# Routing heads and gate stage of a hybrid block: candidates put together a head later, early gathers by half-heads, first product dealt out by contraction steps

## The chip, the cores and the metric

The kernel runs on one core of one Trainium2 chip. The metric is the device time of one execution in microseconds (us), taken as the median of several runs; a profile comes from one further execution.

The engines are named as in the profile: PE is TensorE (PEld its weight loads), DVE is VectorE, ACT is ScalarE, POOL is GpSimd, SP is the engine whose queue issues most loads. Each engine works through its own list of instructions in order and stops at the first one whose inputs or buffers are not ready.

## The reference, cut to what matters

One layer on 512 tokens of 1024 numbers: a normalised mixing block (gating group and banded attention), added to the input, and then a PEER block, which is added too. The change touches the PEER block alone.

```python
def peer_ffn(x, w_query, sub_keys, expert_u, expert_v):
    tokens = x.reshape(-1, 128, d)
    def block(xb):
        q = (xb @ w_query).reshape(128, 8, 2, 128)          # 8 heads, 2 halves
        sc = einsum('thpd,hpkd->thpk', q, sub_keys)         # 128 keys per half
        s_top, i_top = lax.top_k(sc, 16)
        cand = s_top[:, :, 0, :, None] + s_top[:, :, 1, None, :]
        cand_idx = i_top[:, :, 0, :, None] * 128 + i_top[:, :, 1, None, :]
        best, pos = lax.top_k(cand.reshape(128, 8, 256), 16)
        eidx = take_along_axis(cand_idx.reshape(128, 8, 256), pos, -1)
        g = softmax(best, -1)
        u = take(expert_u, eidx, axis=0)                    # 16384 experts of 1024
        h = gelu(einsum('thkd,td->thk', u, xb))
        vv = take(expert_v, eidx, axis=0)
        return einsum('thk,thkd->td', g * h, vv)
```

So every token picks 16 of 16384 experts in each of 8 heads.

## The kernel before, in words

Token tiles have 128 tokens; there are four. Three of them (384 tokens) are computed densely, the first tile by gathering. For the dense tokens the kernel multiplies *all* experts: a first product (x by expert_u, GELU), multiplied by a dense table of gates, and a second product with expert_v. Of those 384 tokens the last 64 are an exception: their first product is not dense (the first product has 320 columns, `NDU`); instead the rows of expert_u that they chose are gathered "early". 64 tokens times 128 choices make 64 gathers of 128 rows, since partitions 64 to 127 hold one half of the choices of these tokens and partitions 0 to 63 the other half.

Experts are worked in tiles of 128, two tiles to a chunk. A tile of the first product is 8 contraction steps (`KT`); each step is three matmuls on a split of the float32 operands into a high and a low part (`mm3`). Before a tile can be multiplied, SP loads it (`raw`), ACT copies the high part (`hi`, L122), and DVE or POOL subtracts to get the low part (`lo`, L123).

Two stages matter here.

The **head stage** (about 225 to 448 us) has one turn per head. `candidates(h)` loads and splits a 1024 by 256 piece of w_query, multiplies it (tiles `pa`), copies the query out (`qt`, ACT L629), multiplies it by the keys (L637), copies the scores out (`scr`, ACT L640) and lets DVE find the 16 best keys of each half (`best_keys`, L551 to L555, tiles `top` and `pos`). Between, it multiplies two tiles of the first product (`pu`, evacuated by ACT as `act`, L534). `pairs` turns the positions into numbers (ACT L568, L569) and adds up the 50 candidates of a head (DVE L576, tile `cand`). In the next turn `choose` finds the 16 best candidates (DVE, tiles `gate` and `bpos`), fills `tree` with copies (POOL L583), makes the bit masks (DVE L589) and picks the expert numbers by six predicated copies (L601) and a copy into `eidx` (L603). Every second turn `indices_early` brings the numbers of two heads for the last 64 tokens into `eu` (a POOL DMA, L494, and an ACT copy, L495); `ready_early` converts them to integers on ACT (L499); `gather_early` issues up to six gathers a turn on POOL (L479, tile `rowe`, 8 buffers), and `dots_early` multiplies each landed row by x and sums (DVE L488). The turns are traced in program order, and a scheduler then sets the order on each engine by priority and by when it expects inputs to be ready. After the last head come eight tiles of the first product as a bridge.

The **gate stage** (about 454 to 635 us) builds the dense table of gates, 8 tokens a step, 48 steps: DVE compares numbers (`bm` L717, `am` L727), POOL multiplies `bm` by the gate (L719), ACT makes two of eight slices of `am`, PE multiplies (L740, into `pa`), ACT copies out (`gst`, L743) and every two steps stores 1 MB to DRAM (L746). `bm` and `am` have three buffers, and PE works two steps behind (`LEAD`). One early gather is issued in each step while some are left, and its dot follows three steps later. Between, 14 tiles of the first product are multiplied: two in the first step and then one whole tile every fourth step, set by `here`, and each multiplied tile is followed by the split of the next. Here the order on PE, DVE, ACT and POOL is the order of the code (`manual_schedule`). After it come six more tiles, and then the second product, which is not changed.

## Time and profile before

| what | value |
|---|---|
| median of 3 runs (lowest, highest) | 1500.43 us (1500.3, 1507.03) |
| the profiled execution's own time | 1508.44 us |
| its span, first to last instruction | 1506.3 us |
| mean granted TensorE clock | 0.978 |
| busy: PE, DVE, ACT, POOL | 1410.9, 1151.1, 645.4, 682.8 us |
| chain that ended last, by engine | PE 35%, DVE 23%, DMA 19%, issue 13%, POOL 7%, ACT 3% |

Read it by stages: PE is busy in 94% of the span, but the second product makes up more than half of that; in the two stages of the change other engines and the DMA take turns at the limit. The profiled execution is 8.0 us longer than the median, and its span is 2.1 us shorter than its time.

### The profile page before, as it was taken

The page shows a single profiled execution, that of the slowest core. Times are in us where ns is not written, and L with a number is a line of the kernel's source. Part 1 is how long each engine was busy: PE and PEld are TensorE (multiplying, and loading weights), DVE is VectorE, ACT ScalarE, POOL GpSimd, SP SyncE. Part 2 cuts the span into 40 slices and gives each one's busy share as a digit, 9 for nine tenths or more (in the row PEclk, how much of TensorE's full clock was granted, in tenths as well). Part 3 has the DMA queues.
Part 4 walks back from the last instruction along what each step waited for, and adds up shares of the span by engine and source line. Part 5 has one row for each costly group of instructions (what it writes and reads, how often), then busy time and mean ns, then how long its engine had stood idle before and what let it go on. Part 6 is the DMA issues. An engine that isn't in the chain of part 4 may idle for free.

```text
span 1506.3 us, 21702 instructions
## 1 busy us (share of the span) xinstructions
PE 1410.9 (94%) x7804; PEld 1241.8 (82%) x7804; DVE 1151.1 (76%) x2345; ACT 645.4 (43%) x1116; POOL 682.8 (45%) x458
## 2 busy tenths in 40 slices
PE   7999999979888788999979999999999999999998
PEld 6886678968877787988968889989898989888877
DVE  4437553779987996578979798898798888788883
ACT  5447534323336766743434333343333333333331
POOL 0000016567748996403525455454555645344520
PEclk9999999989999998999999999999999999999999
DMA  5352225366747996777878899999999999879992
GB/s 181 112 182 70 84 101 194 121 244 217 250 148 220 336 336 184 208 282 276 291 280 294 318 351 343 346 360 348 369 342 349 367 354 377 318 281 328 331 343 99
DMA packets 160907, 396.77 MB, mean 263 GB/s; under 512 B 11792, under 2 KB 74016, under 8 KB 158752
## 3 DMA queue, kind: packets, MB, share of 16 engines
q1 hardware_dynamic: 62992, 197.42, 37.1%
q0 software_dynamic: 46976, 171.50, 30.8%
q10 hardware_dynamic: 50832, 26.48, 6.1%
q8 instruction: 61, 1.00, 0.3%
q14 instruction: 46, 0.38, 0.1%
HBM read 363.86 MB, written 31.46 MB: 262 GB/s over the span
## 4 chain that ended last, share of the span: by engine, by line
PE 35%; DVE 23%; DMA 19%; issue 13%; POOL 7%; ACT 3%; ACTq 0%; DVEq 0%; SPq 0%; POOLq 0%
DMA row<-in_vd,eint 7%; DMA row<-in_ud,eint 6%; PE pu L138 4%; PE pu L140 4%; PE pu L139 4%; DVE lo L123 4%; PE pa L138 3%; PE pa L139 3%; PE pa L140 3%; DVE rowe L488 3%; DVE row L851 2%; PE pa L918 2%; PE pa L919 2%; PE pa L922 2%; POOL row L860 2%
## 5 line engine op out<-in xcount | busy, mean ns | idle before, releaser
L122 ACT ACTIVATE hi<-raw 128x1024 fp32r<-128x1024 f32 x300 | 317.3, 1059 | 508.4 <-DMA raw<-in_vd 194.0
L123 DVE TENSOR_TENSOR lo<-raw,hi 128x1024 fp32r<-128x1024 f32 x251 | 311.4, 1242 | 114.1 <-ACT hi L122 113.2
L860 POOL DMA_INDIRECT row<-in_vd,eint x128 | 201.6, 1575 | 194.7 <-DVE acc L862 159.9
L849 POOL DMA_INDIRECT row<-in_ud,eint x128 | 177.0, 1383 | 201.7 <-DVE row L851 157.4
L140 PE MATMUL pu<-xch,lo 128*128 128x320 f32 x816 | 252.9, 310 | 9.1 <-DVE lo L123 7.1
L138 PE MATMUL pu<-xch,hi 128*128 128x320 f32 x816 | 254.7, 312 | 2.6 <-ACT act L534 2.2
L139 PE MATMUL pu<-xcl,hi 128*128 128x320 f32 x816 | 252.6, 310 | 0.0
L918 PE MATMUL pa<-hi,wh 128*128 128x512 f32 x512 | 200.8, 392 | 0.0
L919 PE MATMUL pa<-lo,wh 128*128 128x512 f32 x512 | 200.2, 391 | 0.0
L862 DVE SCALAR_TENSOR_TENSOR acc<-row,hw,acc 128x1024 f32<-128x1024 f32 x128 | 165.1, 1290 | 42.5 <-DMA row<-in_vd,eint 40.8
L851 DVE SCALAR_TENSOR_TENSOR row<-row,xb 128x1024 f32<-128x1024 f32 x128 | 155.9, 1220 | 36.1 <-DMA row<-in_ud,eint 34.4
L140 PEld LDWEIGHTS pu<-xch,lo 128*128 128x128 f32 x816 | 154.5, 189 | 10.2 <-DVE lo L123 7.9
L138 PEld LDWEIGHTS pu<-xch,hi 128*128 128x128 f32 x816 | 154.8, 190 | 5.8 <-ACT act L534 3.4
L922 PE MATMUL pa<-hi,wl 128*128 128x512 f32 x512 | 158.1, 390 | 0.0
L139 PEld LDWEIGHTS pu<-xcl,hi 128*128 128x128 f32 x816 | 154.5, 189 | 1.6
L123 POOL TENSOR_TENSOR lo<-raw,hi 128x1024 fp32r<-128x1024 f32 x49 | 118.6, 2434 | 79.3 <-ACT hi L122 79.0
L740 PE MATMUL pa<-bm,am 128*128 128x128 f32 x768 | 100.5, 289 | 27.5 <-POOL bm L719 14.5
L740 PEld LDWEIGHTS pa<-bm,am 128*128 128x128 f32 x768 | 94.7, 201 | 32.8 <-POOL bm L719 26.8
L918 PEld LDWEIGHTS pa<-hi,wh 128*128 128x128 f32 x512 | 96.8, 189 | 20.6
L919 PEld LDWEIGHTS pa<-lo,wh 128*128 128x128 f32 x512 | 96.7, 189 | 20.4
L922 PEld LDWEIGHTS pa<-hi,wl 128*128 128x128 f32 x512 | 96.5, 188 | 20.5
L919 PE MATMUL px<-lo,wh 128*128 128x512 f32 x256 | 101.2, 395 | 9.2 <-DVE lo L123 9.1
(216 smaller groups left out, 2620.6 us busy)
## 6 DMA issues: line engine op xcount, KB each, us to landing
raw<-in_uT SPq DMA_DIRECT2D x128, 512.0 KB
raw<-in_vd SPq DMA_DIRECT2D x128, 512.0 KB
gd<-gst ACTq DMA_DIRECT2D x24, 1024.0 KB
gc<-gd SPq DMA_DIRECT2D x15, 1536.0 KB
raw<-in_w_in SPq DMA_DIRECT2D x20, 512.0 KB
raw<-in_wq SPq DMA_DIRECT2D x16, 512.0 KB
raw<-in_w_out SPq DMA_DIRECT2D x8, 512.0 KB
bt<-in_bias SPq DMA_DIRECT2D x8, 256.0 KB
```

The lines of the kernel that those rows point to most:

```text
L122: nc.scalar.activation(hi, raw, AF.Copy)
L123: eng.tensor_tensor(lo, raw, hi.bitcast(F32), op=ALU.subtract)
L138: nc.tensor.matmul(ps, lh[0], rh[0], start=first, stop=False)
L139: nc.tensor.matmul(ps, lh[0], rh[1], start=False, stop=False)
L140: nc.tensor.matmul(ps, lh[1], rh[0], start=False, stop=last)
L740: nc.tensor.matmul(ps[:, i * P:(i + 1) * P], am[:, 4 * q + i, :], bm[:, 4 * q + i, :], start=True, stop=True)
L849: nc.gpsimd.indirect_dma_start(out=row, out_offset=None, in_=ud, in_offset=bass.IndirectOffsetOnAxis(ap=eint[:, j:j + 1], axis=0))
L851: nc.vector.scalar_tensor_tensor(row, row, 1.0, xb0, op0=ALU.mult, op1=ALU.mult, accum_out=hw[:, j:j + 1])
L860: nc.gpsimd.indirect_dma_start(out=row, out_offset=None, in_=vd, in_offset=bass.IndirectOffsetOnAxis(ap=eint[:, j:j + 1], axis=0))
L918: nc.tensor.matmul(accs[t][half], wh[:, b, tok], w[b][0][:, ds_], start=first, stop=False)
L919: nc.tensor.matmul(accs[t][half], wh[:, b, tok], w[b][1][:, ds_], start=False, stop=False)
L922: nc.tensor.matmul(accs[t][half], wl[:, b, tok], w[b][0][:, ds_], start=False, stop=last)
```

## The change

Three edits. `candidates` returns the best keys, and `pairs` is called in the next turn, just ahead of `choose`. The early gathers go by half-heads: the numbers are written as integers straight into `eui`, one half by a converting POOL DMA and the other by a POOL copy, in every turn for the head before, and seven gathers a turn instead of six; the order of the choices in `du` and `dots` follows. And the first product in the gate stage is no longer dealt out by tiles but by contraction steps: `multiply_some` multiplies as many steps of the open tile as the rest needs per remaining step of the loop, and keeps two split tiles ahead (`HELD`).

```diff
-EARLY = 6
+EARLY = 7
+HELD = 2
...
         def indices_early(h):
-            js = slice(h // 2 * TOPK, (h // 2 + 1) * TOPK)
-            nc.gpsimd.dma_start(eu[0:P - UX, js], eidx[P - UX:P, TT - 1, (h + 1) * TOPK:(h + 2) * TOPK])
-            nc.scalar.copy(eu[P - UX:P, js], eidx[P - UX:P, TT - 1, h * TOPK:(h + 1) * TOPK])
+            js = slice(h * HK, (h + 1) * HK)
+            nc.gpsimd.dma_start(eui[0:P - UX, js], eidx[P - UX:P, TT - 1, h * TOPK + HK:(h + 1) * TOPK])
+            nc.gpsimd.tensor_copy(eui[P - UX:P, js], eidx[P - UX:P, TT - 1, h * TOPK:h * TOPK + HK])
         def ready_early(h):
-            js = slice(h // 2 * TOPK, (h // 2 + 1) * TOPK)
-            nc.scalar.copy(eui[:, js], eu[:, js])
-            early.extend(range(js.start, js.stop))
+            early.extend(range(h * HK, (h + 1) * HK))
...
+        def multiply_some(n, whole=False):
+            x2 = (xbh[:, :, T0:T0 + NDU], xbl[:, :, T0:T0 + NDU]) if whole else (xch, xcl)
+            while n > 0 and (open_tile or ready):
+                if not open_tile:
+                    open_tile.extend((*ready.pop(0), pu(), 0))
+                c, b, (hi, lo), ps, k0 = open_tile
+                k1 = min(KT, k0 + n)
+                for k in range(k0, k1):
+                    mm3(ps[:, :NDU], (hi[:, k, :], lo[:, k, :]), [v[:, k, :] for v in x2], k == 0, k == KT - 1)
+                n -= k1 - k0
+                open_tile[4] = k1
+                if k1 == KT:
+                    begun.append((c, b, ps))
+                    open_tile.clear()
...
-            return pairs(rq, top, pos, ND)
+            return top, pos
...
-            if h > 2 and h % 2 == 1:
-                ready_early(h - 3)
+            if h > 1:
+                ready_early(h - 2)
...
-                choose(rq, cands.pop(0), ND, gate[:, GT:, hs], eidx[:, GT:, hs], mask, tree)
-                if h % 2 == 0:
-                    indices_early(h - 2)
+                choose(rq, pairs(rq, *cands.pop(0), ND), ND, gate[:, GT:, hs], eidx[:, GT:, hs], mask, tree)
+                indices_early(h - 1)
...
-                here = LEAD + (AHEAD * BC - i0 - LAST * BC - LEAD) * (n + 1) // steps
-                while split - len(ready) - i0 < min(here, AHEAD * BC - i0 - LAST * BC):
-                    multiply_tile()
+                made = len(ready) * KT + (KT - open_tile[4] if open_tile else 0)
+                left = (AHEAD - LAST) * BC * KT - split * KT + made
+                some = -(-left // (steps + LEAD - n))
+                multiply_some(some)
+                while split < (AHEAD - LAST) * BC + HELD and len(ready) < HELD:
                     split_next(nc.vector if split % 2 else nc.gpsimd)
```

What it does to the order shows in three places. First POOL in the later half of the head stage, before (`lo` is a low part, `rowe` a gathered row, `eu` and `eui` the expert numbers):

```order
L479 DMA rowe<-in_ud,eui 128x1024
L583 COPY tree<-cand 128x1536
L479 DMA rowe<-in_ud,eui 128x1024 x5
L123 TENSOR_TENSOR lo<-raw,hi 128x1024 x3
L479 DMA rowe<-in_ud,eui 128x1024
L123 TENSOR_TENSOR lo<-raw,hi 128x1024
```

and now:

```order
L495 DMA eui<-eidx 64x8
L496 CAST eui<-eidx 64x8
L595 COPY tree<-cand 128x1536
L125 TENSOR_TENSOR lo<-raw,hi 128x1024
L480 DMA rowe<-in_ud,eui 128x1024 x7
L125 TENSOR_TENSOR lo<-raw,hi 128x1024 x3
L480 DMA rowe<-in_ud,eui 128x1024
L125 TENSOR_TENSOR lo<-raw,hi 128x1024
```

Each turn now has a transfer and a conversion of its own ahead of `tree`, and seven or eight gathers stand in one run with the low parts behind them.

On DVE, where one head's best keys end (`top`), the picking of the head before (`tree`) and the sums of the candidates (`cand`) stood so, before:

```order
L555 MAX_INDEX pos_3018<-top_3017,rep_3153 128x8
L601 COPY_PREDICATED tree_3203<-pa_3202,tree_3203 128x48x16
L576 TENSOR_TENSOR cand_3194<-top_3017 128x6x16
L576 TENSOR_TENSOR cand_3194<-top_3017 128x6x8
L576 TENSOR_TENSOR cand_3194<-top_3017 128x6x5
L576 TENSOR_TENSOR cand_3194<-top_3017 128x6x4
L576 TENSOR_TENSOR cand_3194<-top_3017 128x6x3
L576 TENSOR_TENSOR cand_3194<-top_3017 128x6x6
L576 TENSOR_TENSOR cand_3194<-top_3017 128x6x8
```

and stand so now:

```order
L601 TENSOR_TENSOR pa_3464<-bpos_3477,bits_2010 128x288
L566 MAX top_3289<-rep_3425 128x8
L613 COPY_PREDICATED tree_3465<-pa_3464,cand_3468 128x48x18
L567 MAX_INDEX pos_3290<-top_3289,rep_3425 128x8
L613 COPY_PREDICATED tree_3465<-pa_3464,tree_3465 128x48x16
L489 SCALAR_TENSOR_TENSOR rowe_3267,du_2008<-rowe_3267,px_1998 128x1024
L613 COPY_PREDICATED tree_3465<-pa_3464,tree_3465 128x48x8
L489 SCALAR_TENSOR_TENSOR rowe_3269,du_2008<-rowe_3269,px_1998 128x1024
L613 COPY_PREDICATED tree_3465<-pa_3464,tree_3465 128x48x4
L489 SCALAR_TENSOR_TENSOR rowe_3271,du_2008<-rowe_3271,px_1998 128x1024
L613 COPY_PREDICATED tree_3465<-pa_3464,tree_3465 128x48x2
L489 SCALAR_TENSOR_TENSOR rowe_3273,du_2008<-rowe_3273,px_1998 128x1024
```

The sums of the candidates have moved from the start of the picking to its end, behind four early dots; the mask (L601) stands at the end of the keys.

On PE in the gate stage, before, four steps' matmuls (L740, eight to a step) stood between whole tiles of 24 (L138 to L140):

```order
L138 MATMUL pu<-xch,hi 128x320
L139 MATMUL pu<-xcl,hi 128x320
L140 MATMUL pu<-xch,lo 128x320
L740 MATMUL pa<-bm,am 128x128 x32
L138 MATMUL pu<-xch,hi 128x320
L139 MATMUL pu<-xcl,hi 128x320
L140 MATMUL pu<-xch,lo 128x320
```

and now each step's eight are followed by two contraction steps (three in the first twelve steps of the loop):

```order
L751 MATMUL pa<-bm,am 128x128 x8
L140 MATMUL pu<-xch,hi 128x320
L141 MATMUL pu<-xcl,hi 128x320
L142 MATMUL pu<-xch,lo 128x320
L140 MATMUL pu<-xch,hi 128x320
L141 MATMUL pu<-xcl,hi 128x320
L142 MATMUL pu<-xch,lo 128x320
L751 MATMUL pa<-bm,am 128x128 x8
```

The first product's matmuls of the stage are the same in number and only spread. Counted over the whole order, 49 of the 64 early gathers now stand in the head stage and 15 in the gate stage, where it was 36 and 28.

## Rows read from the trace of the kernel before

**Rows 1.** Stretches of both stages: window in us, its length, then busy time (and instructions) of PE, PEld, DVE, ACT and POOL, the granted TensorE clock, the DMA engines' busy share and GB/s.

```profile
343.00:393.00 50.00, 44.41 (x244) 39.98 (x243) 48.44 (x197) 16.44 (x33) 34.51 (x25) 0.97 0.66 221
393.00:448.00 55.00, 48.06 (x285) 45.37 (x284) 54.55 (x213) 18.06 (x33) 35.94 (x22) 0.94 0.58 198
...
470.00:513.00 43.00, 35.37 (x267) 34.00 (x266) 39.56 (x52) 30.03 (x70) 39.71 (x26) 0.97 1.00 316
513.00:563.00 50.00, 43.48 (x329) 41.89 (x327) 46.87 (x59) 34.80 (x79) 45.77 (x30) 0.97 1.04 334
563.00:587.00 24.00, 19.07 (x125) 18.28 (x124) 13.33 (x16) 14.68 (x36) 12.19 (x7) 0.79 0.63 188
587.00:625.00 38.00, 32.81 (x258) 31.59 (x257) 29.58 (x32) 28.76 (x68) 28.47 (x16) 1.00 0.70 201
```

**Rows 2.** Waits in the head stage, 292 to 455 us: the engine and line that waited, what for, us in total, times, the longest.

```profile
ACT top L569 <- DVE pos L555: 15.1, 5, 6.7
...
PE pu L138 <- ACT act L534: 14.2, 3, 7.7
...
DVE rowe L488 <- DMA rowe<-in_ud,eui: 8.5, 2, 8.2
...
DVE ii L693 <- ACT ei L692: 4.6, 1, 4.6
...
DVE top L554 <- DVE top L551: 1.0, 2, 0.6
```

**Rows 3.** Groups of instructions of DVE and POOL in the head stage, 292 to 448 us: busy us, mean ns of one, idle us before them and what ended it.

```profile
L488 DVE SCALAR_TENSOR_TENSOR rowe<-rowe,px 128x1024 f32<-128x1024 f32 x36 | 43.4, 1215 | 8.5 <-DMA rowe<-in_ud,eui 8.5
...
L123 POOL TENSOR_TENSOR lo<-raw,hi 128x1024 fp32r<-128x1024 f32 x25 | 59.4, 2397 | 8.9 <-ACT hi L122 8.7
L479 POOL DMA_INDIRECT rowe<-in_ud,eui x36 | 34.3, 954 | 20.5 <-DVE rowe L488 11.1 <-issue 5.3 <-DVE gate L554 1.3
L583 POOL COPY tree<-cand 128x1536 f32<-128x1536 f32 x6 | 9.0, 1495 | 4.9 <-DVE eidx L603 4.1 <-DVE gate L551 0.8
```

**Rows 4.** The sums of the candidates (L576) and the masks (L589): their groups on DVE in the same stretch, and then the timeline (start, length, both in us) of two of the sums, one mask, and POOL's low parts beside the second sum.

```profile
L576 DVE TENSOR_TENSOR cand<-top 128x48 f32<-128x48 f32 (+5 forms) x42 | 15.4, 434 | 0.0
...
L589 DVE TENSOR_TENSOR pa<-bpos,bits 128x288 uint32<-128x288 uint32 x6 | 5.6, 936 | 0.0
...
300.92 0.88 DVE L576 TENSOR_TENSOR cand<-top 128x96 f32<-128x96 f32 x7
...
374.15 7.13 POOL L123 TENSOR_TENSOR lo<-raw,hi 128x1024 fp32r<-128x1024 f32 x3
...
377.83 4.20 DVE L576 TENSOR_TENSOR cand<-top 128x96 f32<-128x96 f32 x7
...
421.57 2.86 DVE L589 TENSOR_TENSOR pa<-bpos,bits 128x288 uint32<-128x288 uint32 x1
```

**Rows 5.** Timeline of single instructions: the first head's expert numbers, the start of the third head's keys, the first early gather and its dot, the last head's expert numbers, and the gate stage's first comparison.

```profile
282.81 0.24 DVE L603 COPY eidx<-tree 128x48 f32<-128x48 f32 x1
...
292.12 0.49 DVE L551 MAX8 top<-scr 128x8 f32<-128x128 f32 x2 [2.87 <-ACT scr L640]
...
307.65 1.04 POOL L479 DMA_INDIRECT rowe<-in_ud,eui  x1 [0.17 <-ACT hi L122]
...
313.32 1.22 DVE L488 SCALAR_TENSOR_TENSOR rowe<-rowe,px 128x1024 f32<-128x1024 f32 x1 [8.22 <-DMA rowe<-in_ud,eui]
...
447.34 0.23 DVE L603 COPY eidx<-tree 128x48 f32<-128x48 f32 x1
...
454.32 1.22 DVE L717 TENSOR_TENSOR bm<-iota_k,pa 128x1024 f32<-128x1024 f32 x1 [1.76 <-ACT ni L708]
```

**Rows 6.** Timeline: the comparison L717 at the gate stage's steps 15, 28, 34 and 47 (counted from 0 at 454.32).

```profile
512.42 1.21 DVE L717 TENSOR_TENSOR bm<-iota_k,pa 128x1024 f32<-128x1024 f32 x1
...
560.00 1.21 DVE L717 TENSOR_TENSOR bm<-iota_k,pa 128x1024 f32<-128x1024 f32 x1
...
587.72 1.22 DVE L717 TENSOR_TENSOR bm<-iota_k,pa 128x1024 f32<-128x1024 f32 x1
...
624.83 1.22 DVE L717 TENSOR_TENSOR bm<-iota_k,pa 128x1024 f32<-128x1024 f32 x1 [0.71 <-PE pa L740]
```

**Rows 7.** Timeline of PE: the first matmul of a whole tile of the first product, and the next two steps' products behind that tile (a step counts 16 in these records).

```profile
484.89 0.39 PE L138 MATMUL pu<-xch,hi 128*128 128x320 f32 x1
...
488.50 3.73 PE L740 MATMUL pa<-bm,am 128*128 128x128 f32 x32
```

**Rows 8.** Groups of the gate stage, 454 to 628 us: three of DVE and the multiplication on POOL.

```profile
L717 DVE TENSOR_TENSOR bm<-iota_k,pa 128x1024 f32<-128x1024 f32 x48 | 58.2, 1212 | 11.0 <-PE pa L740 9.2 <-ACT ni L708 1.8
L727 DVE TENSOR_TENSOR am<-iota_k,pa 128x768 f32<-128x768 f32 x48 | 45.3, 944 | 0.0
L488 DVE SCALAR_TENSOR_TENSOR rowe<-rowe,px 128x1024 f32<-128x1024 f32 x28 | 33.7, 1210 | 4.1 <-DMA rowe<-in_ud,eui 4.1
...
L719 POOL TENSOR_TENSOR bm<-bm,gt 128x1024 f32<-128x1024 f32 x48 | 90.8, 1899 | 21.4 <-DVE bm L717 19.9
```

**Rows 9.** DMA queues from 470 to 563 us: packets, MB, share of the 16 engines' time in that stretch. q10 carries ACT's stores of gates, q0 POOL's gathers, q1 SP's loads.

```profile
q10 hardware_dynamic: 26406, 13.42, 50.3%
q0 software_dynamic: 3744, 13.63, 40.3%
q1 hardware_dynamic: 864, 3.15, 11.0%
```

More of the change, by code (lines that the diff above doesn't have):

```diff
@@ L49 @@
 HS = NH * TOPK // 2
+HK = TOPK // 2
 NB = 128
@@ L468, in hybrid_block @@
         nc.scalar.copy(xbu[:, 512:], row[:, 512:])
-        eu = gat.tile([P, HS], F32, name="eu")
         eui = gat.tile([P, HS], I32, name="eui")
         du = gat.tile([P, HS], F32, name="du")
-        dots = gat.tile([P, NH // 2, 2, TOPK], F32, name="dots")
+        dots = gat.tile([P, NH, 2, HK], F32, name="dots")
         early, issued = [], []
@@ L522, in split_tile @@
             ready.append((c, b, load_split(uT[i], eng, b=P)))
-        def multiply_tile(whole=False):
-            c, b, (hi, lo) = ready.pop(0)
-            ps = pu()
-            for k in range(KT):
-                x2 = (xbh[:, k, T0:T0 + NDU], xbl[:, k, T0:T0 + NDU]) if whole else (xch[:, k, :], xcl[:, k, :])
-                mm3(ps[:, :NDU], (hi[:, k, :], lo[:, k, :]), x2, k == 0, k == KT - 1)
-            begun.append((c, b, ps))
+        open_tile = []
+        def multiply_some(n, whole=False):
[12 more added lines that the diff above has]
+                    open_tile.clear()
+        def multiply_tile(whole=False):
+            multiply_some(KT, whole)
         def activate_tile():
@@ L674, in hybrid_block @@
         softmax(rq, gate[:, GT:, :].rearrange("p t (h k) -> p (t h) k", k=TOPK), ND * NH)
-        ready_early(NH - 2)
+        ready_early(NH - 1)
         dots_early(0)
@@ L804, in hybrid_block @@
                     gs[t] = gates_of(GT + t, ff.pop(t))
-                here = LEAD + (AHEAD * BC - i0 - LAST * BC - LEAD) * (n + 1) // steps
-                while split - len(ready) - i0 < min(here, AHEAD * BC - i0 - LAST * BC):
-                    multiply_tile()
+                made = len(ready) * KT + (KT - open_tile[4] if open_tile else 0)
[3 more added lines that the diff above has]
+                while split < (AHEAD - LAST) * BC + HELD and len(ready) < HELD:
                     split_next(nc.vector if split % 2 else nc.gpsimd)
-            while ready:
+            while ready or open_tile:
                 if split == AHEAD * BC and not weights:
```

2 lines of the change are left out of this document (1 added, 1 removed).

## The prediction

> **What bounds the kernel now.** I read the table of stretches first [rows 1], then the waits of the head stage, then the groups, the timeline and the DMA queues. The reader is to see four things.
>
> In the later heads DVE is the bound: 48.44 of 50.00 us and 54.55 of 55.00 us busy, with PE at 44.41 and 48.06 [rows 1]. PE's waits there (14.2 us for the evacuation `act`, which ACT had queued behind copies that wait for DVE [rows 2]) are therefore mostly a consequence: whoever frees ACT still finds DVE full.
>
> In the gate stage up to 563 us the DMA engines are the bound, at a share of 1.00 and 1.04 [rows 1], with DVE (46.87 of 50.00) and POOL (45.77) close behind. From 470 to 563 us stores took 50.3% and gathers 40.3% of the DMA time [rows 9].
>
> From 563 to 587 us nothing is the bound. The clock was granted at 0.79 (of the levels 1.2 and 2.4 GHz a mixture), PE was busy for 19.07 of 24.00 us, and DVE for 13.33 [rows 1].
>
> After that, 13 steps (34 to 47) take 624.83 - 587.72 = 37.1 us, 2.85 a step [rows 6]. PE's own work is 3.73 / 2 = 1.87 for a step's products and 488.50 - 484.89 = 3.61 for a tile, a quarter of which falls on a step: 2.77 [rows 7]. So without gathers the stage already runs near PE's pace, lumps or not. What the new dealing can win is the stretch in which it did not.
>
> **The change part by part: the head stage.** 13 of the 28 early gathers of the gate stage [rows 8] move into the head stage, which has 36 [rows 3], with their dots. On DVE, which is the bound there, the end of the stage moves by these terms.
>
> First, the gathers begin a head earlier. The first head's numbers are there at 283.05 [rows 5]; transfer, conversion and `tree` (1.5 us [rows 3]) need about 2.5 us (an estimate), so a first gather starts near 285.5. From its start to its dot the trace shows 313.32 - 307.65 = 5.7 us [rows 5], so the dot starts near 291.2. The order puts three dots and a mask ahead of the third head's keys: 291.2 + 3 x 1.22 + 0.55 = 295.4, where these keys started at 292.12 [rows 5]. That is +3.3.
>
> Second, behind that point stand 46 dots where 36 stood: 10 x 1.22 [rows 3] = +12.2.
>
> Third, DVE waited 8.5 us for the first gathers to land, with nothing else in its queue [rows 2, 3]. With gathers a head earlier this is gone: -8.5.
>
> Fourth, the sums of the candidates. Alone they take 0.88 us a head, but the second one shown took 4.20 and ended just behind POOL's three low parts (374.15 + 7.13 = 381.28) [rows 4]. All six together took 15.4, which is 15.4 - 6 x 0.88 = 10.1 too much. One mask took 2.86, where the other five have (5.6 - 2.86) / 5 = 0.55 [rows 4]: 2.3 too much. In the new order POOL mostly stands at the expert numbers and at `tree`, which wait for DVE, while DVE does the sums, so most of the 10.1 should go. The masks, however, now come at the end of the keys, when POOL has just issued its run of seven or eight gathers and turns to up to three low parts in a row. A mask caught there costs up to 7.13 - 0.55 = 6.6. The bounds of what remains are 0 and, for five heads, 33. I take 8, near what was there (12.4), since one mask in four or five should be caught: -4.4.
>
> This is where a page of the Trainium skill speaks against the change. "SBUF — State Buffer", section "Who interferes with whom", says that a DVE instruction with two inputs in SBUF contends with a GpSimd instruction that reads SBUF, and that whoever holds the shared pair holds it for the whole instruction. The trace agrees: 4.20 beside 0.88 for the same sums, while dots, which have one input in SBUF, stay at 1215 ns. By that rule each mask is a matter of who starts first; a rival below follows from it.
>
> Fifth, keys beside gathers have short waits: 1.0 us over two heads [rows 2]. With gathers beside nearly all keys I add 0.7 for four more heads: +3.
>
> Sum: 3.3 + 12.2 - 8.5 - 4.4 + 3 = +5.6. The expert numbers of the last head would be ready at about 453.2 instead of 447.57.
>
> POOL gets more too, in one queue: two gathers more a head, a transfer of its own and a conversion. Its work per head is 4 x 2.40 + 8 x (0.95 + 0.15 of issue) + 1.5 and under 1 for the numbers, about 20.7 [rows 3], against a DVE turn of 24 or more. That fits, if with little room. The conversion waits for landed gathers; behind it stand `tree` and the low parts, which PE wants a head later.
>
> ACT loses eight small copies; I cost that at nothing, since ACT is busy for a third of these stretches [rows 1]. The candidates put together later move ACT's position copies behind the second `act` in the later heads, so that PE's 14.2 us [rows 2] should mostly go; DVE is the bound, so that is worth nothing by itself.
>
> **The passage to the gate stage.** From the last expert numbers to the first comparison it took 454.32 - 447.57 = 6.75 us [rows 5], 4.6 of them DVE waiting for ACT's conversion `ei` [rows 2], which stood behind a copy of early numbers and the last `act` of the bridge. The copy is gone, and PE's bridge tiles end before a DVE that ends later. I keep 3.35 of 6.75: -3.4. The bounds are 0 and -4.6.
>
> **The gate stage.** Before, the first comparison is at 454.32 and the last (step 47) at 624.83 [rows 5, 6], 170.5 us.
>
> Steps with a gather were DMA work of 0.503 x 93 / 13.42 x 0.524 MB = 1.83 for the store, 0.403 x 93 / 13.63 x 0.524 = 1.44 for the gather and 0.11 x 93 / 3.15 x 0.524 = 1.70 for a tile's load, a quarter of it per step: 3.70 [rows 9]. Measured from step 15 to 28: 47.6 / 13 = 3.66 [rows 6]. It fits.
>
> Now only 15 steps have a gather. For the first twelve, three contraction steps fall on a step, so 3/8 of a load: 1.83 + 1.44 + 0.64 = 3.91; then 3.70. That is 12 x 3.91 + 3 x 3.70 = 58.0, the same as the 58.1 that the first 15 steps took. The double tile at the start, which held up step 1, gives way to a DMA that is full from the beginning. DVE (1.21 + 0.94 + 1.21 = 3.36) and POOL (1.90 + 1.10 and a share of low parts) fit beneath [rows 3, 8].
>
> The other 32 intervals, to step 47, have no gather. Their price has two bounds: 2.85 from steps 34 to 47, and (624.83 - 560.00) / 19 = 3.41 from all steps without gathers [rows 6], which contain the bad stretch. That stretch, steps 28 to 34, took 27.7 us where 6 x 2.85 = 17.1 would do. Even dealing should take away what starts it (PE held by a whole tile while POOL, DVE and ACT wait in turn), but three late dots and the change of token tile stay. I take 3.05: 32 x 3.05 = 97.6. Sum 155.6, so -14.9; with the bounds -21.3 and -3.4.
>
> What follows (six tiles, the second product) is the same work and starts earlier by the sum.
>
> **The sum.** +5.6 - 3.4 - 14.9 = -12.7 us. The profiled execution took 1508.4, so one like it would take 1495.7. The median of the runs shown is 8.0 lower, 1500.4, and from it I forecast 1487.7, rounded to 1488.
>
> **The rivals.** *Both halves go well.* No mask is caught (-8) and the steps run at 2.85 (-6.4): 1473. For it: PE already reaches that pace. Against: DVE's turn leaves POOL only a few us, and a turn that slips meets low parts.
>
> *Moved, not removed.* The dealing wins nothing beyond the gathers, and steps without them stay at 3.41: -3.4 instead of -14.9, so 1499. For it: the last 13 steps show that lumps cost little. Against: the stretch at 563 us followed a lump.
>
> *The masks (slower).* Every mask of five heads falls behind three low parts: 33 us instead of 8, 25 more, so 1513. For it: one already did for 2.86, and the sums show that DVE gets no turn between low parts in a row. It outweighs the rest from 4 us a head on; more than 20 us over the forecast make the kernel slower by over 0.5%. Against: a late DVE also holds POOL at the expert numbers, which puts the two back in step. This is the case that the page named above speaks for.
>
> *It doesn't do what it says* would be ACT still standing at DVE's keys ahead of `act`; the order shows the copies directly behind it, so that PE has one `act` more in hand. I give that no time of its own, as DVE is the bound.
>
> **How the numbers follow.** Forecast 52% (its own range 1478 to 1496), both halves well 20%, moved 16%, masks 12%. A difference under 0.5%, 7.5 us, can't be told from none for this kernel. Faster by more than that (under 1493): 20 + 47 of the 52 = 67%. Within: the other 5 and 15 of the 16 = 20%. Slower: 12 + 1 = 13%. The range, 1470 to 1505, leaves out the masks and a little at either end.
>
> **What would show it.** Right: the third head's keys start near 295; sums of 0.9 us everywhere; DVE's wait for the first rows near zero; last expert numbers at 448 to 458; 3.9 us a step in the first 12 steps with a DMA share near 1.0, and about 3.0 behind them without a stretch at a low clock. Wrong: masks of 3 to 7 us; POOL busy without a gap in the heads; heads longer than 25 us; steps over 3.4 us once the gathers have ended.

## The result and the profile after

The changed kernel took 1497.4 us in the median of ten runs (1488.07 to 1504.97), the kernel before, beside it, 1504.1 us (1500.3 to 1513.96): ratio 0.9949, with a 95% interval of 0.9928 to 0.9971. That is faster by 6.7 us in the medians, and by 7.7 if the ratio is taken. The forecast was 1488 from 1500.43, 12.4 us less and a ratio of 0.9917, which lies below the interval: right in direction, too large in size.

The two profiled executions differ by more than that (spans 1506.3 and 1487.9 us), so I first cut both into the same four stretches. The rows are, in this order: from the first head's keys to the last expert numbers, from there to the first comparison `bm`, from there to the second product, and the second product. Columns as in [rows 1]. Before:

```profile
252.67:447.34 194.67, 174.43 (x974) 158.72 (x973) 171.45 (x770) 64.28 (x124) 125.84 (x80) 0.95 0.58 199
447.34:454.32 6.98, 4.98 (x34) 4.47 (x32) 0.60 (x5) 3.03 (x9) 0.79 (x2) 1.00 0.00 1
454.32:653.70 199.38, 167.32 (x1221) 161.44 (x1219) 151.37 (x175) 132.01 (x293) 144.70 (x90) 0.95 0.85 268
653.70:1500.20 846.50, 826.40 (x4304) 729.05 (x4305) 703.21 (x1128) 314.16 (x446) 383.94 (x260) 0.99 0.87 320
```

The changed kernel:

```profile
250.82:451.41 200.59, 178.09 (x988) 162.30 (x987) 187.99 (x796) 63.25 (x118) 142.08 (x104) 0.95 0.65 227
451.41:456.45 5.04, 2.96 (x20) 2.45 (x18) 0.59 (x5) 2.46 (x7) 0.98 (x3) 1.00 0.02 0
456.45:641.30 184.85, 159.28 (x1202) 153.59 (x1200) 137.34 (x150) 129.56 (x291) 132.10 (x77) 0.97 0.81 250
641.30:1481.40 840.10, 829.15 (x4324) 731.89 (x4325) 706.36 (x1128) 315.03 (x448) 387.57 (x260) 0.99 0.87 323
```

The head stage is 5.9 us longer (forecast +5.6), the passage 1.9 shorter (-3.4), the gate stage with the tiles behind it 14.5 shorter (-14.9). All three look like the forecast. But the second product, which I had called the same work, is 6.4 shorter, and the first keys start 1.85 us earlier, ahead of anything that was changed. One trace is not enough to judge by; the runs below gave two more.

In the head stage the groups of DVE from 292 to 452 us answer to [rows 3, 4]:

```profile
L489 DVE SCALAR_TENSOR_TENSOR rowe<-rowe,px 128x1024 f32<-128x1024 f32 x47 | 57.3, 1224 | 0.0
...
L601 DVE TENSOR_TENSOR pa<-bpos,bits 128x288 uint32<-128x288 uint32 x7 | 16.5, 2353 | 0.0
...
L588 DVE TENSOR_TENSOR cand<-top 128x48 f32<-128x48 f32 (+5 forms) x42 | 8.3, 254 | 0.0
```

From 292 us on the dots no longer wait (0.0 where 8.5 stood); the first two, now ahead of this window, still waited 5.1 us for their rows. The sums have fallen from 15.4 to 8.3 us, and the masks have risen from 5.6 (six of them) to 16.5 (seven). The timeline shows these two dots, and then one mask just ahead of POOL's run of three low parts and one behind the start of such a run. Then come the points that answer to [rows 5, 6]: last expert numbers, first comparison, steps 15 and 47.

```profile
287.75 1.22 DVE L489 SCALAR_TENSOR_TENSOR rowe<-rowe,px 128x1024 f32<-128x1024 f32 x1 [4.14 <-DMA rowe<-in_ud,eui]
...
289.90 1.22 DVE L489 SCALAR_TENSOR_TENSOR rowe<-rowe,px 128x1024 f32<-128x1024 f32 x1 [0.92 <-DMA rowe<-in_ud,eui]
...
292.32 0.46 DVE L601 TENSOR_TENSOR pa<-bpos,bits 128x288 uint32<-128x288 uint32 x1
...
293.17 7.12 POOL L125 TENSOR_TENSOR lo<-raw,hi 128x1024 fp32r<-128x1024 f32 x3
...
342.94 7.10 POOL L125 TENSOR_TENSOR lo<-raw,hi 128x1024 fp32r<-128x1024 f32 x3
...
343.60 6.77 DVE L601 TENSOR_TENSOR pa<-bpos,bits 128x288 uint32<-128x288 uint32 x1
...
451.41 0.23 DVE L615 COPY eidx<-tree 128x48 f32<-128x48 f32 x1
...
456.45 1.22 DVE L728 TENSOR_TENSOR bm<-iota_k,pa 128x1024 f32<-128x1024 f32 x1 [1.76 <-ACT ni L719]
...
516.40 1.22 DVE L728 TENSOR_TENSOR bm<-iota_k,pa 128x1024 f32<-128x1024 f32 x1
...
618.53 1.22 DVE L728 TENSOR_TENSOR bm<-iota_k,pa 128x1024 f32<-128x1024 f32 x1
```

A mask that starts 0.85 us before POOL's run takes 0.46 us and is over before it; one that starts 0.66 us behind it takes 6.77, to the end of the run and a little on (342.94 + 7.10 = 350.04). In the gate stage the first 15 steps took 516.40 - 456.45 = 59.95 us (forecast 58.0) and the other 32 took 102.13, 3.19 a step (forecast 3.05).

### The profile page after: what moved, and what is told of

Same layout as the page of the kernel before. It is cut to its first block, busy times and chain, and to the rows that moved or that the text cites. A ratio compares the mean times of both kernels' runs of the same rounds, so it can differ in the third digit from the quotient of the medians.

```text
span 1487.9 us, 21702 instructions
## 1 busy us (share of the span) xinstructions
PE 1403.9 (94%) x7804; PEld 1235.9 (83%) x7804; DVE 1158.7 (78%) x2345; ACT 641.9 (43%) x1108; POOL 690.4 (46%) x470
## 4 chain that ended last, share of the span: by engine, by line
PE 51%; DVE 19%; DMA 13%; issue 7%; POOL 5%; ACT 4%; ACTq 0%; SPq 0%; DVEq 0%; POOLq 0%
PE pu L140 6%; PE pu L142 6%; PE pu L141 6%; PE pa L932 5%; PE pa L933 5%; PE pa L936 5%; DMA row<-in_vd,eint 5%; DVE rowe L489 3%; PE px L933 3%; PE px L932 3%; PE px L936 3%; DMA row<-in_ud,eint 3%; PE pa L140 2%; PE pa L141 2%; PE pa L142 2%
## 5 line engine op out<-in xcount | busy, mean ns | idle before, releaser
L874 POOL DMA_INDIRECT row<-in_vd,eint x128 | 196.9, 1538 | 196.8 <-DVE acc L876 165.2
L863 POOL DMA_INDIRECT row<-in_ud,eint x128 | 184.6, 1442 | 190.3 <-DVE row L865 149.1
L140 PE MATMUL pu<-xch,hi 128*128 128x320 f32 x816 | 257.7, 316 | 3.5 <-ACT act L546 2.9
L865 DVE SCALAR_TENSOR_TENSOR row<-row,xb 128x1024 f32<-128x1024 f32 x128 | 156.3, 1223 | 28.9 <-DMA row<-in_ud,eint 28.5
L140 PEld LDWEIGHTS pu<-xch,hi 128*128 128x128 f32 x816 | 154.7, 190 | 7.2 <-ACT act L546 5.0
L932 PEld LDWEIGHTS pa<-hi,wh 128*128 128x128 f32 x512 | 96.8, 189 | 20.6
L936 PEld LDWEIGHTS pa<-hi,wl 128*128 128x128 f32 x512 | 96.6, 189 | 20.6
```

The costliest lines, as they stand in the source:

```text
L140: nc.tensor.matmul(ps, lh[0], rh[0], start=first, stop=False)
L863: nc.gpsimd.indirect_dma_start(out=row, out_offset=None, in_=ud, in_offset=bass.IndirectOffsetOnAxis(ap=eint[:, j:j + 1], axis=0))
L874: nc.gpsimd.indirect_dma_start(out=row, out_offset=None, in_=vd, in_offset=bass.IndirectOffsetOnAxis(ap=eint[:, j:j + 1], axis=0))
L932: nc.tensor.matmul(accs[t][half], wh[:, b, tok], w[b][0][:, ds_], start=first, stop=False)
L936: nc.tensor.matmul(accs[t][half], wl[:, b, tok], w[b][0][:, ds_], start=False, stop=last)
```

## The experiments

**Each edit alone, and all three again.** Three kernels take one edit each; the fourth is the changed kernel, unaltered.

```text
 pairs_only      pairs() called in the next turn; the rest as before
 gathers_only    half-heads, EARLY = 7; the rest as before
 deal_only       multiply_some(); the rest as before
```

> The kernel before with the third edit alone: the first product of the gate stage dealt out by contraction steps. The 28 early gathers of the gate stage stay. Theory (each edit brings its own term, and they add): the 28 steps with a gather stay bound by the DMA (12 x 3.91 + 16 x 3.70), the other 19 intervals fall to 3.05, so 164 us from the first comparison to the last instead of 170.5, and about one whole tile (3.6 us) less is left behind the last comparison: 6 to 10 us faster, ratio 0.9935 to 0.996. Rival (the gathers carry it: dealing helps only where the DMA is not full): first comparison to second product at 196 to 199 us as before (199.4), ratio 0.998 to 1.000.

> The kernel before with the second edit alone: early gathers by half-heads, seven a turn; candidates put together and first product dealt as before. Theory (terms add): the head stage grows by +10 (the +5.6 of the forecast and the 4.4 of contention that only the later candidates take away), the passage to the gate stage loses 2 to 3, the gate stage loses 13 gathers' worth of DMA time, 13 x (3.66 - 3.41) to 13 x (3.66 - 3.05) = 3 to 8 us: together -1 to +4 us, ratio 0.999 to 1.003. Rival (the gathers carry the whole gain): ratio 0.995 or less, with the gate stage at 186 us or less from first comparison to second product.

> The kernel before with the first edit alone: the candidates of a head put together in the next turn. Theory (terms add): the sums of the candidates no longer meet POOL's low parts (-10.1 us of contention), masks at the end of the keys meet some of them instead (up to 8), nothing else moves: 0 to 4 us faster, ratio 0.997 to 1.000. Rival (the later candidates are the step that loses time, by the masks): masks of 6 to 7 us twice or more, 3 to 8 us slower, ratio 1.002 to 1.005.

> All three edits, the changed kernel itself, a second time, beside its parts. Theory (terms add): ratio within the interval already measured, 0.993 to 0.997, and equal to the product of the three parts' ratios; in the trace two masks of 6 to 7 us, head stage about 200 us from the first keys to the last expert numbers, first comparison to second product about 185 us. Rival (one edit carries it): the ratio of one part alone is as low as this one.

Measured: dealing alone 0.9916 (0.9893 to 0.994), gathers alone 1.0007 (0.9985 to 1.0029), later candidates alone 1.0006 (0.9982 to 1.0031), all three 0.9963 (0.9942 to 0.9985). The product of the parts would be 0.9929; it lies under the interval of the whole. So the edits don't simply add, and dealing alone carries more than all three together, as the rival of the last expectation said. The dealing did better than its range. The gathers met theirs by luck: their head stage grew by 23 us, not 10, and passage and gate stage fell by 14, not 5 to 11. The later candidates alone left the sums at 13.6 us from 280 us on (16.2 before), where 10 us less were expected. The gate stage of dealing alone is 190.3 us although all 28 gathers are still in it, that of the gathers alone 188.0, of the later candidates alone 196.2, of all three 186.2. The head stage is 195.2 with dealing alone (194.7 before), but 218.0 with the gathers alone, whose traced run was the slowest of its twelve (1517.18, median 1507.42).

The changed kernel's second trace differs from its first in the head stage: 212.2 us instead of 200.6. Its masks took 23.8 us instead of 16.5, and the timeline shows the first long one beginning with POOL's run, at the same hundredth of a microsecond:

```profile
296.17 7.09 POOL L125 TENSOR_TENSOR lo<-raw,hi 128x1024 fp32r<-128x1024 f32 x3
...
296.17 7.42 DVE L601 TENSOR_TENSOR pa<-bpos,bits 128x288 uint32<-128x288 uint32 x1
```

From the first head's expert numbers to the second's it is 34.9 us here and 27.1 in the first trace: the 7 us of this one mask, and little else.

**The mask's second input.** Six small instructions a head take the place of each mask, in two forms with almost the same order on DVE and the same order on POOL and PE: in one the bit is a constant of the instruction, in the other (the control) it is read from SBUF. The last three lines are those of the control.

```diff
-            nc.vector.tensor_tensor(mask.rearrange("p (l n) -> p l n", l=6),
...
+            for i in range(6):
+                nc.vector.tensor_scalar(mask.rearrange("p (l n) -> p l n", l=6)[:, i, :],
+                                        bpos.rearrange("p t k -> p (t k)"),
+                                        1 << i, None, op0=ALU.bitwise_and)
...
+                nc.vector.tensor_tensor(mask.rearrange("p (l n) -> p l n", l=6)[:, i, :],
+                                        bpos.rearrange("p t k -> p (t k)"),
+                                        bits[:, i:i + 1].to_broadcast([P, n * TOPK]), op=ALU.bitwise_and)
```

> The changed kernel with each mask made by six small DVE instructions that have one input in SBUF (the bit is a constant of the instruction) instead of one with two. Theory M (masks caught behind POOL's low parts are what makes the head stage long: 13 us over their own time in the first trace of the changed kernel, 20 in the second): masks of about 0.7 us a head, head stage from the first keys to the last expert numbers 186 to 196 us instead of 201 and 212, ratio 0.984 to 0.990. Rival (DVE's turn is full anyway: what the masks give back goes into waits for scores, gathers or the other two-input sums): head stage still over 198, ratio 0.993 to 0.997.

> Control for the run with one input: the same six small instructions a head in nearly the same order, but each reads the bit from SBUF, so each has two inputs there. Theory M: pieces of a mask still take 2 to 7 us where POOL's low parts run in a row, head stage 200 us or more, 8 to 20 us longer than the one with one input; ratio 0.993 to 0.999. Rival (the order that the pieces bring, not the second input, makes the difference): the same time as with one input within 3 us.

Measured: 1500.89 us, 0.9976 (0.9955 to 0.9997), with one input, and 1519.67 us, 1.011 (1.008 to 1.014), with two. The groups of DVE from 280 to 480 us, with one input:

```profile
L588 DVE TENSOR_TENSOR cand<-top 128x48 f32<-128x48 f32 (+5 forms) x49 | 23.7, 521 | 0.0
L602 DVE TENSOR_SCALAR pa<-bpos 128x48 uint32<-128x48 uint32 x44 | 9.0, 204 | 0.2
```

and with two:

```profile
L602 DVE TENSOR_TENSOR pa<-bpos,bits 128x48 uint32<-128x48 uint32 x42 | 33.7, 802 | 0.2
L588 DVE TENSOR_TENSOR cand<-top 128x48 f32<-128x48 f32 (+5 forms) x49 | 14.0, 320 | 0.0
```

With one input no piece is held up (204 ns in the mean, 0.21 us at most, though 12 of the 48 began beside a low part of POOL); with two, single pieces took up to 7.2 us. The head stages are 212.2 and 224.4 us, 12.2 apart, and the control is the slower one as theory M says, though its ratio lies above the 0.993 to 0.999 expected. But the kernel with one input missed its range, in the way that its rival named: the sums of the candidates, which still have two inputs, were caught in the masks' place (23.7 us where the changed kernel has 8.9 from 280 us on). Freeing one of two kinds of instruction that can be held up moved the loss to the other.

The first and third edit without the moved gathers, with these masks of one input:

> The first and third edit without the second (early gathers as before, six a turn, by pairs of heads), with the masks of one input. Theory (early gathers in the head stage cost as much as they save in the gate stage): head stage 181 to 188 us, first comparison to second product 188 to 191, ratio 0.984 to 0.988, not above the changed kernel with masks of one input. Rival (once the masks are free the moved gathers pay): at least 0.3% slower than the changed kernel with masks of one input.

Measured 0.9927 (0.9897 to 0.9957), 1492.79 us: below the changed kernel with the same masks, but out of the range, for the same reason (sums 20.6 us); its head stage is 194.2.

**Both inputs out of POOL's way.** ACT copies what the sums and the mask need into the PSUM tile that already holds the mask. DVE's instructions stay the same in kind and number, though the scheduler places some of them elsewhere in a turn.

```diff
+                one = side.rearrange("p (a t r) -> p a t r", a=2, t=n)
+                nc.scalar.copy(one[:, 0], top[:, 0, :, 0, :])
+            nc.scalar.activation(one[:, 1], pos[:, :, 0, :], AF.Copy, scale=float(NK))
...
+                                        one[:, :, i:j, None].to_broadcast(full), op=ALU.add)
...
+                ps = pa()
+                mask = ps[:, 0:6 * ND * TOPK].bitcast(U32)
+                side = ps[:, 6 * ND * TOPK:8 * ND * TOPK]
+                bit = ps[:, 8 * ND * TOPK:8 * ND * TOPK + 6].bitcast(U32)
+                nc.scalar.copy(bit, bits)
```

> The changed kernel with one input of each two-input DVE instruction of the heads taken out of SBUF: ACT copies the first halves' best scores, their scaled positions and the mask bits into the PSUM tile that holds the mask, and the sums of the candidates and the masks read them there. DVE's instructions stay the same in kind and number. Theory M (sums and masks caught behind POOL's low parts set how long the head stage is): masks about 0.5 us and sums 0.9 us a head, 11 us together instead of 26 to 33, and the head stage shorter by that difference, 184 to 190 us; ratio 0.981 to 0.987. Rival (DVE would lose the time in other waits, for scores, gathers or POOL's copies into the tree): head stage 195 us or more, ratio 0.990 or more.

> The changed kernel with these inputs in PSUM, a second time, beside it. Theory (its runs lie close because nothing is left to chance in the heads): 1477 to 1482 us in all runs, ratio 0.980 to 0.985, masks of 0.46 us. Rival (the narrow spread was luck): a spread of over 10 us, as the changed kernel's.

> The first edit alone, with the sums' and masks' second input in PSUM: the kernel before without the contention, and without the second and third edit. Theory (the contention is the only term that was mis-sized; the others hold): without it the moved gathers cost the head stage +10 (3.3 + 12.2 - 8.5 + 3), the passage and the gate stage give 3.4 and 14.9, the second product some 5, so this kernel is 8 to 14 us slower than the changed kernel with the same inputs: ratio 0.988 to 0.993. Rival (dots and keys in the heads were mis-sized too): less than 5 us slower, or faster, than the changed kernel with the same inputs, ratio 0.986 or less.

> The changed kernel a third time, for its spread. Theory (what differs between runs is how many masks are caught): masks take 13 to 25 us in this trace, and the head stage is 200 to 215 us, longer by what the masks take more than the 16.5 us of the first trace, within 5 us; runs spread over 10 us or more. Rival (the head stage varies by waits for gathers and scores): head stage and masks do not move together.

Measured: the changed kernel with these inputs 1478.86 us, 0.9825 (0.9799 to 0.985), and again 1479.28, 0.985 (0.9807 to 0.9892); the first edit alone with them, which is the kernel before with the later candidates and without the contention, 1490.27, 0.9892 (0.9848 to 0.9936); the changed kernel a third time 1501.89, 0.9976 (0.9949 to 1.0002). In the first of these, groups of DVE from 280 to 450 us:

```profile
L592 DVE TENSOR_TENSOR cand<-top,pa 128x48 f32<-128x48 f32 (+5 forms) x49 | 7.1, 191 | 0.0
L605 DVE TENSOR_TENSOR pa<-bpos,pa 128x288 uint32<-128x288 uint32 x8 | 3.7, 457 | 0.0
```

and a mask in the middle of a run of POOL:

```profile
304.06 7.11 POOL L125 TENSOR_TENSOR lo<-raw,hi 128x1024 fp32r<-128x1024 f32 x3
...
308.20 0.46 DVE L605 TENSOR_TENSOR pa<-bpos,pa 128x288 uint32<-128x288 uint32 x1
```

The same instruction at the same kind of place takes 0.46 us instead of 7. It is the only one of the eight masks of this trace that began beside a low part; of the 56 small instructions that make the sums 23 did, and none of those took over 0.25 us. POOL's low parts are neither faster nor slower for it (7.11). The head stage is 195.6 and 193.0 us, not the 184 to 190 expected, although sums and masks fell to 10.8: by the stretches DVE is busy for 171.90 of 195.61 us there and PE for 178.23, so DVE is no longer the bound and part of what was freed becomes a wait, as the rival had it (195 us or more), while the time came out as the theory had it. The gain of 20 us in the median came from the head stage (208 in the mean of the three traces of the changed kernel, 194 now), the passage (5.6, now 3.0) and the second product.

The pair with and without the second and third edit, both free of the contention, gives those edits' worth by itself. The four stretches of the first edit alone:

```profile
253.03:436.53 183.50, 172.84 (x1001) 157.41 (x999) 157.48 (x771) 67.31 (x142) 126.21 (x80) 0.99 0.62 211
436.53:439.57 3.04, 1.34 (x5) 0.97 (x5) 0.64 (x3) 2.13 (x6) 1.01 (x2) 0.50 0.02 4
439.57:637.10 197.53, 166.93 (x1222) 161.51 (x1221) 148.66 (x176) 132.19 (x294) 143.83 (x90) 0.95 0.86 270
637.10:1486.20 849.10, 828.50 (x4303) 729.13 (x4304) 704.02 (x1128) 313.83 (x446) 392.09 (x260) 0.99 0.87 319
```

and of the changed kernel with the same inputs:

```profile
252.19:447.80 195.61, 178.23 (x1001) 161.44 (x999) 171.90 (x798) 66.03 (x135) 142.20 (x104) 0.97 0.70 233
447.80:450.84 3.04, 1.35 (x5) 0.98 (x5) 0.63 (x5) 2.14 (x6) 1.12 (x3) 0.50 0.03 1
450.84:634.20 183.36, 158.85 (x1201) 152.91 (x1200) 135.88 (x150) 129.50 (x291) 131.95 (x77) 0.97 0.81 252
634.20:1472.50 838.30, 828.30 (x4324) 730.26 (x4325) 705.38 (x1128) 315.05 (x448) 395.84 (x260) 1.00 0.87 323
```

Head stage +12.1 (+9.5 against the second trace of that kernel; expected +10), passage 0.0 (-3.4), gate stage -14.2 (-14.9), second product -10.8 (-5). In the medians it is -11 us, inside the expected 8 to 14, with two misses in it that cancel; by the ratios it is 6.3 us, and the two intervals overlap. So the moved dots, keys and gathers were sized about right in the stages, while the rival's less than 5 us in all is unlikely and not excluded.

The changed kernel's third trace has masks of 23.6 us and a head stage of 211.8, as the second. In all traces of kernels with the moved gathers the head stage goes with sums and masks together (from 280 us on): 25.4 and 200.6, 32.4 and 212.2, 32.7 and 211.8; with late low parts (below) 26.0 and 200.8; with pieces of one input 32.7 and 212.2, the gathers alone 39.6 and 218.0, the control 47.7 and 224.4. It is not one for one: between the first trace of the changed kernel and the other two, 7 us of masks and sums go with 11 to 12 us of head stage, and the rest stays open. The narrow spread of the kernel with inputs in PSUM (1478.6 to 1481.0 the first time) was 1476.7 to 1486.6 the second, so "nothing left to chance" goes too far: its spread is 10 us there, against 13 for the changed kernel beside it and 14 for the first edit alone with these inputs.

**The low parts of the gate stage one step later.** In [rows 3] and the gate stage alike a low part stands behind ACT's high part. This edit issues it one step after its load.

```diff
-                    split_next(nc.vector if split % 2 else nc.gpsimd)
+                    split_next(nc.vector if split % 2 else nc.gpsimd, lows)
...
+                while lows:
+                    lows.pop(0)()
```

> The changed kernel with the low part of a split tile in the gate stage put one step later in the queues of DVE and POOL than its load and its high part. Theory L (DVE standing at a low part for ACT's high part, 26.8 us in 8 waits, is what keeps the steps without gathers at 3.2 us instead of 2.85): these waits shrink to under 8 us, first comparison to second product 177 to 181 us instead of 185 to 186, time 4 to 7 us under the changed kernel's own. Rival (PE waits for POOL's multiplication and is 85 to 92% busy; whoever frees DVE only moves the wait): 184 to 187 us, time that of the changed kernel within 2 us.

> The third edit of the change alone, with the low parts of the gate stage one step later. Theory L: 4 to 7 us under the third edit alone, ratio 0.986 to 0.989. Rival (with a gather in 28 steps the DMA sets the pace and hides the low parts): ratio 0.990 to 0.993.

> The same with the low parts of the gate stage one step later too. Theory (the two add): head stage as in the run before, first comparison to second product 176 to 181 us, ratio 0.976 to 0.983. Rival (PE and DMA take up one of the two): no more than 2 us under the better of the two single edits.

> The same two edits on the first and third edit of the change alone, with early gathers as before (36 in the head stage, 28 in the gate stage). Theory (moved gathers cost the heads what they save the gate stage, 10 dots of 1.2 us against 13 steps bound by the DMA): within 0.3% of the run with all three edits. Rival (they pay once DVE is free of the contention): at least 0.4% slower than that run.

DVE's waits in the changed kernel's gate stage (what waited, for what, us, times, longest):

```profile
DVE lo L125 <- ACT hi L124: 26.8, 8, 5.7
DVE bm L728 <- PE pa L751: 8.3, 5, 2.6
```

and with the low parts a step later:

```profile
DVE lo L124 <- ACT hi L123: 14.7, 7, 6.8
DVE bm L727 <- PE pa L750: 7.7, 8, 2.6
```

The waits did not shrink to 8 us, but the stage did as expected: 177.9 us from the first comparison to the second product instead of 184.9. The run took 1491.5 us, 0.991 (0.9877 to 0.9942), 6 to 10 us under the changed kernel's three medians; its interval overlaps with those of the first two. On dealing alone the same edit gave 1489.51, 0.9895 (0.9864 to 0.9926), where dealing alone had 0.9916: between the two expectations, with a gate stage of 185.6 instead of 190.3, so by the traces a stage with 28 gathers does not hide the low parts altogether, while the intervals of the two ratios overlap.

With both edits, inputs in PSUM and late low parts, the changed kernel took 1470.03 us, 0.9756 (0.9729 to 0.9783); without the second edit of the change, 1473.33, 0.9785 (0.9759 to 0.981). The two add, and the first of these beats both kernels, by 2.4% the one before. The moved gathers are worth 3 us in the medians, which the intervals do not tell from nothing, and by the stretches of the two traces they cost 5 us: head stage 192.7 against 182.7, gate stage 179.0 against 186.1, second product 839.2 against 836.5. With masks of one input the kernel without them was the faster by 8 us (1492.79 against 1500.89). So no pair of runs here shows that the second edit pays.

## Why the prediction was right in direction and too large

| stretch | forecast | first trace | second | third |
|---|---|---|---|---|
| head stage | +5.6 | +5.9 | +17.5 | +17.1 |
| passage | -3.4 | -1.9 | -1.2 | -1.0 |
| first comparison to second product | -14.9 | -14.5 | -13.2 | -14.2 |
| second product | 0 | -6.4 | -3.5 | -3.2 |
| sum | -12.7 | -16.9 | -0.4 | -1.3 |

Each column is a trace of the changed kernel less the one trace of before, whose run took 1508.44. The traced runs themselves took 1489.67, 1509.07 and 1508.12 us, the ends of a spread whose medians are 1497.4 to 1501.9; the ratios of the two repeats were 0.9963 and 0.9976, the last with an interval that holds 1.

**The step that failed is the fourth of the head stage**, "I take 8, near what was there (12.4), since one mask in four or five should be caught: -4.4". The sums did go back to nearly their own time (8.6 to 9.1 us from 280 us on), though not by the later candidates alone, which left them at 13.6. But masks of over 5 us came twice in seven in the first trace and three times in the second and third, with a fourth of 2.6. Sums and masks together went from 24.2 us before (8.0 + 16.2 from 280 us on) to 25.4, 32.4 and 32.7: +1.2, +8.2 and +8.5 instead of -4.4. That is a miss of 6 to 13 us, which is as much as the 5 to 6 that the result lacks, or more. In the first trace it does not show, since DVE's other waits fell more than I had allowed: busy time grew by 187.99 - 171.45 = 16.5, idle time shrank from 23.2 to 12.6. In the other two busy time grew by 23.6 and 23.8 and idle time shrank by 6.1 and 6.7.

The Trainium skill, "SBUF — State Buffer", section "Who interferes with whom", has the rule by which it goes: a DVE instruction with two inputs in SBUF contends with a GpSimd instruction that reads SBUF, one with at most one, outside the modes that use both ports, does not, and the order of issue decides who waits. The traces agree on the first two: 7.42 us at 296.17, and 0.46 at 308.20 within a run too, with an input in PSUM. On the third they are divided. In the changed kernel's second product a low part of DVE that began 0.15 us ahead of a POOL copy kept its 1.22 us, and the copy took 1.98 instead of 1.06:

```profile
820.62 1.22 DVE L125 TENSOR_TENSOR lo<-raw,hi 128x1024 fp32r<-128x1024 f32 x1
820.77 1.98 POOL L595 COPY tree<-cand 128x1024 f32<-128x1024 f32 x1 [0.39 <-DVE row L865]
...
918.61 1.06 POOL L595 COPY tree<-cand 128x1024 f32<-128x1024 f32 x1
```

But in the kernel before a low part of DVE took 4.23 us although it began at 461.13, 0.74 us ahead of POOL's at 461.87.

I gave this contention of the masks the rival's 12% and priced my own forecast as if a mask came at a random moment. It does not. The order puts the mask at the end of the keys and dots, where POOL comes to the end of its issues: in three or four of the seven heads of each trace a mask and a run of low parts began within a microsecond of each other, and small shifts decide over up to 7 us at a time. That is the masks' rival come true in good part: 13 to 20 us over the masks' own time, where it said 33 for all.

**The rest of the head stage** held. Behind the first rows the dots no longer wait; for those rows DVE still waited 4.3 to 5.3 us, where "near zero" was named as the sign of being right. The start of the third head's keys came 2.4 us later against the first head's in the first trace (forecast 3.3), and 10.3 in the other two, where a mask that was held up stands ahead of it. With the contention taken away on both sides the remaining terms measure +9.5 to +12.1 against +10.

**The passage** gave 1.0 to 1.9 of its 3.4: DVE still waited 2.7 to 3.6 us for ACT's conversion. With the inputs in PSUM the passage took 3.04 us with the copy of early numbers and without it, so taking that copy away, for which the forecast counted 3.4, is not shown to bring anything.

**The gate stage** came out by luck, by errors that cancel. To the last comparison it took 162.1 us where the forecast had 155.6: -8.4 instead of -14.9. The steps without gathers took 3.19 instead of 3.05, since low parts on DVE wait for ACT, which the forecast had not looked at; moving them a step later brought the same 32 steps to 94.7 us, 2.96 a step (part of this only moved: the tail behind them grew from 22.8 to 26.6 us). Against that, the tail behind the last comparison fell from 28.9 to 22.8 us, since 44 contraction steps of the first product (132 matmuls) stood there before and some 33 (100 matmuls) now, which I had called the same work. Nor does the gain of the stage belong to the dealing: alone it gave -9.0, the fewer gathers alone -11.4, all three edits together -13 to -14.5, so each takes part of the other's. With the gathers alone, and whole tiles as before, the 32 steps already took 3.23 us each, against 3.19 with the dealing. There the rival "moved, not removed" was nearly right about what the dealing adds, though not about its price of 3.41.

**The second product** was no part of the forecast and got shorter: 835.6 to 844.7 us in all traces of kernels with the third edit, 846.1 to 850.3 in all without. In the waits of PE over 100 us of it, from 753.7 us on, the kernel before shows:

```profile
PE pu L140 <- DVE lo L123: 6.9, 2, 5.6
PE px L919 <- DVE lo L123: 6.2, 4, 2.3
```

and the changed kernel, from 741.3 us on:

```profile
PE px L933 <- DVE lo L125: 3.1, 2, 2.9
PE pu L140 <- ACT act L546: 2.1, 2, 1.7
PE pu L142 <- DVE lo L125: 0.7, 2, 0.4
```

Over the whole of the second product PE's waits for DVE's low parts come to 16.2 us before and 7.9 now. The code of that stage is unchanged, but the scheduler set another order for DVE: in the traces its instructions stand there in one order in all four kernels without the third edit, and in another in all kernels with it (those with masks in pieces aside). That this order is the cause was not tried by itself. The shorter stage is worth 3 to 6 us here, without which the result would have been nearer to no change; of the 13 us that dealing alone gained it is 5.9.

The baseline took its part as well: the three runs shown had a median of 1500.43, while the medians beside the later runs lie at 1504 to 1506. In ratios it doesn't matter.

## What to carry to other kernels

Before moving a small DVE instruction with two inputs in SBUF, look at what POOL does at its new place: behind the start of a back-to-back run of POOL instructions that read SBUF it waited here for the whole run (6.77 and 7.42 us for 0.46), and the order of a turn can bring both to the same moment in half of the turns. Take one input out of SBUF (PSUM here) for all such instructions at once; freeing one kind alone moved the loss to the other. And when a sum of stages is forecast, cut at a point where the same work is left on either side, and take the changed kernel's order in the stages behind it into account, even where their code is the same.

## What was not expected of the hardware

That a DVE instruction gets no turn between POOL's low parts in a row was in the prediction, read from the sums; the masks show how far it goes: 7.42 us for 0.46 of its own beside three low parts of 2.4 us, where waiting for one would have cost 2.4. A gap of 0.32 us between two low parts is enough for a turn: in the kernel before, a mask that began at 285.48, 0.31 us behind the start of one, took 2.42 us and ended as the next began.

What the prediction did not have is that the same program gives head stages of 200.6, 212.2 and 211.8 us in three executions: a shift of under a microsecond decides whether a mask is over before POOL's run (0.85 us ahead of it) or waits for all of it (with it). How much of this kernel's spread of 13 to 17 us between runs comes from that is not shown: the kernel before spread as much, and the first edit alone with its inputs in PSUM, where no mask and no sum is held up, still spread 14 us over six runs.
